# Four 32-row column tiles per expert, 32 token slots, and weight rows in 8 KB runs, in a two-block transformer kernel with 32 routed experts

## The chip, the cores and the metric

The kernel runs on one core of one Trainium2 chip. The metric is device time in microseconds (us) of one execution. TensorE does the matrix products (PE in the profile, PEld for its weight loads), VectorE is DVE, ScalarE is ACT, GpSimd is POOL, and SyncE (SP) issues nearly all transfers from HBM to the on-chip memory, the SBUF. Matrix products accumulate in PSUM.

## The reference

A first transformer block (two layers of three attention kinds) is followed by a second one with modulation vectors, banded attention, and a mixture of experts. All arithmetic is float32; 256 tokens of width 2048. The part that the change touches:

```
def hier_moe(h, w_rg, b_rg, w_re, b_re, w_gate, w_up, w_down):
    t = h.reshape(-1, D_MODEL)                       # 256 x 2048
    g_logits = t @ w_rg + b_rg                       # 4 groups, the best one is taken
    e_logits = (t @ w_re + b_re).reshape(n_tok, 4, 8)
    ...                                              # the best 2 of the 8 experts in that group
    for e in range(N_EXPERTS):                       # 32
        a = jax.nn.silu(t @ w_gate[e]) * (t @ w_up[e])
        y = y + combine[:, e:e + 1] * (a @ w_down[e])
```

Each token goes to two experts, so an expert gets 16 tokens on average. `w_gate[e]` and `w_up[e]` are 2048 x 512, `w_down[e]` is 512 x 2048, 4.19 MB each: 12.58 MB an expert, 402.7 MB in all, read once.

## The kernel before

The first block, the attention of the second and its output projection run up to about 1405 us. They split every weight into two parts and multiply three times. Beside them SP also streams the modulation matrix (`ada_gen`), which DVE multiplies. Then come the experts, one after the other.

**Slots.** A router gives each token a rank within each of its experts. Every expert has `CAP` = 64 slots. `gather` (line 1292) builds a one-hot matrix from the ranks for the two experts of a pair (2 x 64 = 128 columns), and `quarter` multiplies it with the token matrix `x`, four 128-row pieces of the model width at a time, into the tile `xg`. DVE and ACT apply norm, scale and shift, and the result is `xe` (or `xet`), the transposed input of both experts. Tokens beyond `CAP` slots are left to `overflow` (line 1393), a loop over all experts behind a branch that is taken only when some expert has more than `CAP` tokens. The branch stands after the fifth pair.

**Expert products.** `expert_gu` (line 1336) runs over 16 pieces of the model width. For each it multiplies the 64 slots with the gate piece into PSUM rows 0 to 63 and with the up piece into rows 64 to 127: two column tiles of TensorE, each with its own weights streaming through. A float32 product is two instructions in the trace. ACT copies the result out, four transposes (`guT`) turn it, and ACT and DVE form silu(gate) x up (`eth`, `aT`). `down` (line 1360) multiplies that with the four 128-row pieces of `w_down`, again in two column tiles of 64 (`acc`), and DVE scales the result into `y`. After both experts of a pair `combine` (line 1370) multiplies the 128 slot rows with the routing weights `C` (tile `cb`) and DVE adds them to the tokens' sum.

**Weights.** `load_gu` (line 1133) loads 1 MB tiles of four pieces: partition p gets rows p, 128+p, 256+p and 384+p, each a 2 KB run. `load_d` loads 512 KB tiles with 4 KB runs. There are nine 1 MB places for gate and up (an expert needs eight) and eight 512 KB places for down (an expert needs eight). SP issues the loads in one fixed order and waits, before each, until the products that used the place have run. The first 5.24 MB of expert 0 are loaded during the output projection. The order on each engine is written by a scheduler that follows the program's order within limits.

**End.** The last expert's down weights come in three column strips (line 1462), so that the final norm can follow strip by strip.

## Time and profile before

| | us |
|---|---|
| median of three runs | 2483.78 (2482.15 to 2483.81) |
| the profiled execution | 2481.46 |
| its span in the trace | 2479.8 |

The profiled execution's own time is 1.7 us above its span, and the median is 2.3 us above the profiled execution. The profile page gives busy times of each engine, 40 slices of the span, the chain of work that ended last, and the costliest groups. The trace also answers for windows: for each stretch the busy time of every engine with its number of instructions, the granted clock of TensorE (1.00 is 2.4 GHz, 0.50 is 1.2 GHz), the busy share of the 16 DMA engines (overlapping packets can bring it above 1) and the GB/s they moved.

### The profile page before, as it was taken

The numbers are of one execution on the slowest core, as the hardware profiler recorded it, in microseconds if no ns is written. First come the engines' busy times: TensorE is split into PE (matmuls) and PEld (weight loads), VectorE is DVE, ScalarE is ACT, GpSimd is POOL, SyncE is SP. The second block draws the span as 40 slices with busy tenths as digits, with TensorE's granted clock in tenths as the row PEclk, the third lists the DMA queues.
The fourth block names the chain that finished last, engine by engine and source line by source line (L and its number), as shares of the span: only waits on it lengthen the run. The fifth ranks groups of instructions, "written<-read, shape, count | busy, mean of one in ns | idle before, by whom it ended". The sixth has DMA issues, their size and how long they took to land. (4 is left out here: it accounts for less than half of the span.)

```text
span 2479.8 us, 34810 instructions
## 1 busy us (share of the span) xinstructions
PE 2344.6 (95%) x13428; PEld 1603.6 (65%) x13428; DVE 1344.5 (54%) x2207; ACT 847.7 (34%) x1727; POOL 99.3 (4%) x148
## 2 busy tenths in 40 slices
PE   8999999999999999899999899999899999999997
PEld 8998986799988877887877644333333333333342
DVE  5776867877767777867777821222222222222234
ACT  5553635555435355454565211111111111111111
POOL 0000100000100000202010000000000000000000
PEclk9999999999999999999999899999999999999998
DMA  6677986777888978769758899999999999999994
GB/s 219 221 241 249 303 280 231 271 255 234 260 263 261 290 241 280 242 234 306 250 198 298 311 358 373 394 394 394 342 394 391 393 390 389 390 394 394 394 376 177
DMA packets 340019, 760.98 MB, mean 307 GB/s; under 512 B 27628, under 2 KB 48472, under 8 KB 339848
## 3 DMA queue, kind: packets, MB, share of 16 engines
q1 hardware_dynamic: 334728, 750.92, 85.3%
q0 software_dynamic: 4928, 7.70, 1.3%
q8 instruction: 107, 1.75, 0.3%
q14 instruction: 64, 0.52, 0.1%
q10 hardware_dynamic: 192, 0.08, 0.0%
HBM read 755.69 MB, written 2.97 MB: 306 GB/s over the span
## 5 line engine op out<-in xcount | busy, mean ns | idle before, releaser
L265 ACT CAST hl<-raw 128x1024 fp32r<-128x1024 f32 (+4 forms) x478 | 423.9, 897 | 518.0 <-PE acc L290 237.5
L266 DVE TENSOR_TENSOR hl<-raw,hl 128x1024 fp32r<-128x1024 f32 (+4 forms) x478 | 485.4, 1032 | 102.9 <-ACT hl L265 102.3
L290 PE MATMUL acc<-xT,hl 128*128 128x256 f32 x3744 | 473.8, 286 | 7.7 <-DVE hl L266 4.2
L290 PEld LDWEIGHTS acc<-xT,hl 128*128 128x128 f32 x3744 | 458.0, 193 | 15.6 <-ACT hl L265 6.3
L529 DVE SCALAR_TENSOR_TENSOR ada<-raw,cact,ada 128x1024 f32<-128x1024 f32 x240 | 308.2, 1290 | 156.4 <-DMA raw<-in_w_ada_dram 138.8
L1345 PE MATMUL gu<-ew,xe 128*64 128x512 f32 x1526 | 344.1, 595 | 0.0
L1363 PE MATMUL acc<-ew,aT 128*64 128x512 f32 x992 | 237.2, 624 | 20.6 <-DVE aT L1357 20.6
L1345 PEld LDWEIGHTS gu<-ew,xe 128*64 128x64 f32 x1526 | 106.0, 137 | 203.8 <-issue 184.0
L294 PE MATMUL acc<-hl,mT 128*128 128x512 f32 x768 | 187.8, 397 | 0.6 <-DVE hl L266 0.6
L1355 DVE SCALAR_TENSOR_TENSOR eth<-eth,guT 128x256 f32<-128x256 f32 x32 | 13.5, 421 | 314.3 <-ACT eth L1354 314.3
L294 PE MATMUL acc<-hl,xT 128*128 128x512 f32 (+1 forms) x768 | 161.8, 371 | 18.1 <-DVE hl L266 17.8
L1326 PEld LDWEIGHTS xg<-oh,xres 128*128 128x128 f32 x1024 | 130.8, 196 | 72.2 <-issue 64.6
L290 PE MATMUL acc<-hT,hl 128*128 128x256 f32 x1248 | 168.9, 289 | 2.1 <-DVE hl L266 2.1
L1348 ACT COPY gus<-gu 128x512 f32<-128x512 f32 x32 | 18.8, 586 | 443.9 <-PE gu L1345 438.5
L1332 ACT ACTIVATE xe<-xe,modc 128x128 f32<-128x128 f32 x192 | 64.2, 392 | 308.7 <-DVE xe L1331 308.6
L1363 PEld LDWEIGHTS acc<-ew,aT 128*64 128x64 f32 x992 | 68.9, 142 | 148.3 <-issue 109.7
L290 PEld LDWEIGHTS acc<-hT,hl 128*128 128x128 f32 x1248 | 155.8, 192 | 12.5 <-issue 9.9
L294 PEld LDWEIGHTS acc<-hl,mT 128*128 128x128 f32 x768 | 142.1, 189 | 33.7 <-issue 4.0
L294 PEld LDWEIGHTS acc<-hl,xT 128*128 128x128 f32 x768 | 133.8, 194 | 45.3 <-DVE hl L266 23.3
L1331 DVE SCALAR_TENSOR_TENSOR xe<-xg,modc,rsb 128x128 f32<-128x128 f32 x192 | 56.2, 344 | 182.8 <-PE xg L1326 182.8
L1326 PE MATMUL xg<-oh,xres 128*128 128x128 f32 x1024 | 145.6, 287 | 5.0 <-ACT rsb L1306 5.0
L1368 DVE TENSOR_TENSOR y<-acc,gt2A 64x512 f32<-64x512 f32 x93 | 63.9, 687 | 144.4 <-PE acc L1363 142.8
(333 smaller groups left out, 2283.5 us busy)
## 6 DMA issues: line engine op xcount, KB each, us to landing
ew<-in_w_up_dram SPq DMA_DIRECT2D x128, 1024.0 KB, 11.5
ew<-in_w_down_dram SPq DMA_DIRECT2D x256, 512.0 KB, 10.2
ew<-in_w_gate_dram SPq DMA_DIRECT2D x125, 1024.0 KB, 11.7
raw<-in_w_in_dram SPq DMA_DIRECT2D x248, 512.0 KB, 5.1
raw<-in_w_ada_dram SPq DMA_DIRECT2D x192, 512.0 KB, 5.1
raw<-in_w_out_dram SPq DMA_DIRECT2D x96, 512.0 KB, 5.4
raw<-in_w_ada_final_dram SPq DMA_DIRECT2D x64, 512.0 KB, 5.9
raw<-in_w_in_dram SPq DMA_DIRECT2D x32, 256.0 KB, 3.7
```

The costliest lines, as they stand in the source:

```text
L265: A.copy(dst_hi, src)
L266: V.tensor_sub(dst_lo, src, dst_hi)
L290: T.matmul(acc[:m, b, o : o + 256], w[:, u, c : c + m], xk[v], start=st, stop=last and j == 2, skip_group_check=True)
L294: T.matmul(acc[:, b, o : o + m], xk[v][:, P * tb : P * tb + P], w[:, u, c : c + m], start=st, stop=last and j == 2, skip_group_check=True)
L529: V.scalar_tensor_tensor(ah, raw, ck, ah, op0=OP.mult, op1=OP.add)
L1326: T.matmul(ps[:, m * j : m * j + m], x[:, tb, P * k : P * k + P], oh[:, tb, :], start=j + tb == 0, stop=tb == 1, skip_group_check=True)
L1331: V.scalar_tensor_tensor(dst, ps[:, m * j : m * j + m], G2[:, k : k + 1], rs, op0=OP.mult, op1=OP.mult)
L1332: A.activation(dst, dst, AF.Identity, bias=m2[:, k : k + 1])
L1345: T.matmul(ps[64 * v : 64 * v + 64, :], xe(i, k)[:, CAP * b : CAP * b + CAP], gu(v, k), start=k == 0, stop=k == KT - 1, skip_group_check=True)
L1348: A.copy(g, ps)
L1363: T.matmul(acc[64 * (s % 2) : 64 * (s % 2) + 64, s // 2, :], aT[:, f, :], wd(f, s), start=f == 0, stop=f == 3, skip_group_check=True)
L1368: V.tensor_mul(yv(i, s)[64 * b : 64 * b + 64, :], acc[h, s // 2, :], gt2(s)[h, :])
```

## The change

`CAP` becomes 32, so four experts fill 128 columns, and the pair becomes a quad. `gather` and `combine` run once for four experts, with the same shapes as before. The gather of the next quad is asked for inside the last expert of the present one. `expert_gu` uses four column tiles of 32: gate and up, each for an even and an odd piece, so that the even and the odd sums stand in different PSUM rows. A product with the constant matrix `fold` takes the place of the four transposes: it turns the tile and adds the two sums. `down` uses four column tiles, one for each 512 columns of the output.

The model width is cut differently. Piece k no longer holds rows 128k to 128k+127 but, within each group of 512 rows, every fourth one (`quads`), so that partition p needs four neighbouring rows of `w_gate` or `w_up`, one run of 8 KB. For that the transposes of `x` before the router, the gather, the router's weights and the modulation columns use the same cut; `x` is then read in steps of four elements. `overflow` stands after the third quad and would take seven rounds an expert where it took three. Expert 0's early tiles hold 4, 4, 4, 3, 3 and 2 pieces, as many in all as before.

```
-CAP = 64
+CAP = 32
+NQ = P // CAP
...
+    def quads(t, k):
+
+        return t[..., 512 * (k // 4) : 512 * (k // 4) + 512].rearrange("p (c j) -> p j c", j=4)[:, k % 4, :]
...
+    def mod_quads(v0, gname):
+
+        rows = wk.tile([12, 512], F32, tag="stage", bufs=3, name=uid("mquad"))
+        nc.gpsimd.dma_start(rows[0:8, :], modd[v0 : v0 + 2, :].rearrange("v (m c) -> (v m) c", m=4))
+        nc.gpsimd.dma_start(rows[8:12, :], a[gname][0].rearrange("(m c) -> m c", m=4))
+        ps = pt.tile([P, 512], F32, tag="tp", name=uid("mqc"))
...
-    mod_cols(3)
+    gffn = mod_quads(3, "g_ffn_2")
     m2 = modc[3]
     G2 = modc[4]
-    V.scalar_tensor_tensor(G2, G2, 1.0, cols("g_ffn_2", KT), op0=OP.add, op1=OP.mult)
-    nc.sync.dma_start(wr[:, :, 0:4], a["w_router_group_2"][0].rearrange("(k p) n -> p k n", p=P))
-    nc.sync.dma_start(wr[:, :, 4:36], a["w_router_expert_2"][0].rearrange("(k p) n -> p k n", p=P))
+    V.scalar_tensor_tensor(G2, G2, 1.0, gffn, op0=OP.add, op1=OP.mult)
+    for c0, c1, nm in ((0, 4, "w_router_group_2"), (4, 36, "w_router_expert_2")):
+        src = a[nm][0].rearrange("(m p j) n -> p m j n", p=P, j=4)
+        for m_ in range(4):
+            nc.sync.dma_start(wr[:, 4 * m_ : 4 * m_ + 4, c0:c1], src[:, m_])
...
+    def gu_rows(w, m):
+
+        return w[512 * m : 512 * m + 512, :].rearrange("(p j) n -> p j n", j=4)
...
-            src = a[("w_gate_2", "w_up_2")[v]][0, e, P * k0 : P * (k0 + nk), :].rearrange("(k p) n -> p k n", p=P)
-            if pre:
-                t = pslot([P, nk, 512], F32, uid("ewp"))
-                nc.sync.dma_start(t, src)
-            else:
-
-                t = eload(src, [P, nk, 512], "xm" if e == 1 and k0 == 0 else None)
+            w = a[("w_gate_2", "w_up_2")[v]][0, e]
+
+            t = pslot([P, nk, 512], F32, uid("ewp")) if pre else etile([P, nk, 512], "xm" if e == 1 and k0 == 0 else None)
+            k = k0
+            while k < k0 + nk:
+                n = min(4 - k % 4, k0 + nk - k)
+                nc.sync.dma_start(t[:, k - k0 : k - k0 + n, :], gu_rows(w, k // 4)[:, k % 4 : k % 4 + n, :])
+                k += n
...
-                    T.transpose(ps[:, j, P * tb : P * tb + P], x[:, tb, P * k : P * k + P], ident)
+                    T.transpose(ps[:, j, P * tb : P * tb + P], quads(x[:, tb, :], k), ident)
...
-                    T.matmul(ps[:, m * j : m * j + m], x[:, tb, P * k : P * k + P], oh[:, tb, :], start=j + tb == 0,
+                    T.matmul(ps[:, m * j : m * j + m], quads(x[:, tb, :], k), oh[:, tb, :], start=j + tb == 0,
...
-    def expert_gu(i, b, gu, quarter=None):
+    def expert_gu(i, b, gu, quarter=None, nxt=None):
+
 
         ps = pss.tile([P, 512], F32, tag="s", name=uid("gu"))
         if quarter:
             quarter(0)
-        for k in range(KT):
+        for k in range(0, KT, 2):
             if quarter and k % 4 == 0 and k < 12:
                 quarter(k // 4 + 1)
             for v in range(2):
-                T.matmul(ps[64 * v : 64 * v + 64, :], xe(i, k)[:, CAP * b : CAP * b + CAP], gu(v, k),
-                         start=k == 0, stop=k == KT - 1, skip_group_check=True)
+                for d in range(2):
+                    c = CAP * (2 * v + d)
+                    T.matmul(ps[c : c + CAP, :], xe(i, k + d)[:, CAP * b : CAP * b + CAP], gu(v, k + d),
+                             start=k == 0, stop=k == KT - 2, skip_group_check=True)
+            if nxt and k % 4 == 2:
+                nxt(k // 4)
...
-            T.transpose(ps[:, P * f : P * f + P], g[:, P * f : P * f + P], ident)
-        v4 = ps.rearrange("p (f c) -> p f c", f=4)
+            T.matmul(ps[:, 2 * CAP * f : 2 * CAP * f + 2 * CAP], g[:, P * f : P * f + P], fold, start=f == 0, stop=True,
+                     skip_group_check=True)
+        v4 = ps[:, : 8 * CAP].rearrange("p (f c) -> p f c", f=4)
...
-    def down(acc, aT, wd, i, b, fs, ss):
-        for f in fs:
-            for s in ss:
-                T.matmul(acc[64 * (s % 2) : 64 * (s % 2) + 64, s // 2, :], aT[:, f, :], wd(f, s),
-                         start=f == 0, stop=f == 3, skip_group_check=True)
-        if fs[-1] == 3:
-            for s in ss:
-                h = slice(64 * (s % 2), 64 * (s % 2) + 64)
-                V.tensor_mul(yv(i, s)[64 * b : 64 * b + 64, :], acc[h, s // 2, :], gt2(s)[h, :])
+    def down(acc, aT, wd, i, b):
+
+        for f in range(4):
+            for s in range(4):
+                T.matmul(acc[CAP * s : CAP * s + CAP, 0, :], aT[:, f, :], wd(f, s), start=f == 0, stop=f == 3,
+                         skip_group_check=True)
+        for s in range(4):
+            h = slice(CAP * s, CAP * s + CAP)
+            V.tensor_mul(yv(i, s)[CAP * b : CAP * b + CAP, :], acc[h, 0, :], gt2(s)[h, :])
...
+    fold = cp.tile([P, 2 * CAP], F32, name="fold")
+    idq = ident.rearrange("p (v d c) -> p v d c", v=2, d=2)
+    V.tensor_add(fold.rearrange("p (v c) -> p v c", v=2), idq[:, :, 0, :], idq[:, :, 1, :])
...
-    LAST = NE // 2 - 1
-    for pr in range(LAST + 1):
-        i = pr % 2
-        C, quarter = gather(slot[:, :, 2 * pr : 2 * pr + 2], comb[:, :, 2 * pr : 2 * pr + 2], i, 2)
-        aTs = []
-        for b in range(2):
-            e = 2 * pr + b
+    def quad(q):
+        return gather(slot[:, :, NQ * q : NQ * q + NQ], comb[:, :, NQ * q : NQ * q + NQ], q % 2, NQ)
+
+    LAST = NE // NQ - 1
+    C, quarter = quad(0)
+    for q in range(LAST + 1):
+        i = q % 2
+        for b in range(NQ):
+            e = NQ * q + b
             gw = gu0 if e == 0 else gu1 if e == 1 else load_gu(e, GU) if e > 2 else {**gu2, **load_gu(2, GU[2:])}
             if e == 0:
                 gu1 = load_gu(1, GU)
                 gu2 = load_gu(2, GU[:2])
-            aT = expert_gu(i, b, lambda v, k: gw[v, k], None if b else quarter)
-            aTs.append(aT)
+            nxt = None
+            if b == NQ - 1 and q < LAST:
+                C_next, nxt = quad(q + 1)
+            aT = expert_gu(i, b, lambda v, k: gw[v, k], None if e else quarter, nxt)
...
+            if e == NE - 3:
...
-        if pr == 4:
+                combine(C, i, P, s, lambda tb: y[tb], q == 0)
+            C = C_next
+        if q == 2:
...
-        m = n // 2
+        m = n // 4
...
-            for v in range(2):
-                T.matmul(ps[64 * v : 64 * v + 64, :], aTs[1][:, f, :], wd[f // nf][:, f % nf, m * v : m * v + m], start=f == 0,
+            for v in range(4):
+                T.matmul(ps[CAP * v : CAP * v + CAP, :], aT[:, f, :], wd[f // nf][:, f % nf, m * v : m * v + m], start=f == 0,
                          stop=f == 3, skip_group_check=True)
-        for v in range(2):
```

On PE, a stretch of one expert's gate and up products before, and the transposes behind them (`gu` is the PSUM tile, `ew2409` a gate tile of four pieces, `ew2410` an up tile, `xe` the gathered input; the first two rows come four times before the next tiles' turn):

```order
L1345 MATMUL gu2415_15354<-ew2409_15342,xe2191_14248 64x512
L1345 MATMUL gu2415_15354<-ew2410_15344,xe2191_14248 64x512
...
L1345 MATMUL gu2415_15354<-ew2411_15346,xe2191_14248 64x512
L1345 MATMUL gu2415_15354<-ew2412_15348,xe2191_14248 64x512
...
L1351 MATMUL guT2417_15389<-ident_80,gus2416_15387 128x128 x4
```

The same place now (`x2` stands for two matmuls in a row; the first two rows come twice):

```order
L1376 MATMUL gu2463_15552<-ew2457_15540,xe2190_14257 32x512 x2
L1376 MATMUL gu2463_15552<-ew2458_15542,xe2190_14257 32x512 x2
...
L1376 MATMUL gu2463_15552<-ew2459_15544,xe2190_14257 32x512 x2
L1376 MATMUL gu2463_15552<-ew2460_15546,xe2190_14257 32x512 x2
...
L1384 MATMUL guT2465_15587<-fold_14284,gus2464_15585 128x64 x4
```

A weight tile still takes four matmuls, each now for 32 columns of the array instead of 64; four in a row go to four different column tiles. The four products behind them stream 64 columns instead of 128.

On PE, the end of a pair before, between the down products of its second expert (`acc`) and the first products of the next pair, with the next pair's gather (`xg`) and the combining (`cb`) between them:

```order
L1363 MATMUL acc2428_15415<-ew2427_15413,aT2419_15397 64x512 x2
L1326 MATMUL xg2452_15504<-oh2437_15460,xres_78 128x128 x5
L1373 MATMUL cb2429_15436<-y2193_14251,C2379_15165 128x512
L1373 MATMUL cb2430_15439<-y2193_14251,C2379_15165 128x512
L1326 MATMUL xg2452_15504<-oh2437_15460,xres_78 128x128 x2
L1326 MATMUL xg2453_15529<-oh2437_15460,xres_78 128x128 x2
...
L1373 MATMUL cb2436_15457<-gtB_13334,C2379_15165 128x512
L1345 MATMUL gu2450_15486<-ew2442_15470,xe2190_14247 64x512
```

The gather's new place, among the down products of a quad's third expert:

```order
L1384 MATMUL guT2465_15587<-fold_14284,gus2464_15585 128x64 x4
L1331 MATMUL rs2487_15654<-oh2485_15650,rstd2189_14205 128x128 x2
L1354 MATMUL xg2491_15669<-oh2485_15650,xres_78 128x128 x2
L1398 MATMUL acc2476_15613<-ew2468_15597,aT2467_15595 32x512 x2
L1398 MATMUL acc2476_15613<-ew2469_15599,aT2467_15595 32x512 x2
L1354 MATMUL xg2491_15669<-oh2485_15650,xres_78 128x128 x2
L1398 MATMUL acc2476_15613<-ew2470_15601,aT2467_15595 32x512 x2
L1354 MATMUL xg2491_15669<-oh2485_15650,xres_78 128x128 x4
```

The next quad's gather is done one expert before it is needed, and only the combining still stands between a quad's last down products and the next quad.

On SP, one expert's loads before:

```order
L1125 DMA ew2411_15346<-in_w_gate_2_dram 128x4x512
L1125 DMA ew2412_15348<-in_w_up_2_dram 128x4x512
L1125 DMA ew2413_15350<-in_w_gate_2_dram 128x4x512
L1125 DMA ew2414_15352<-in_w_up_2_dram 128x4x512
L1125 DMA ew2420_15399<-in_w_down_2_dram 128x1024
```

and now:

```order
L1169 DMA ew2459_15544<-in_w_gate_2_dram 128x2048
L1169 DMA ew2460_15546<-in_w_up_2_dram 128x2048
L1169 DMA ew2461_15548<-in_w_gate_2_dram 128x2048
L1169 DMA ew2462_15550<-in_w_up_2_dram 128x2048
L1148 DMA ew2468_15597<-in_w_down_2_dram 128x1024
```

Their number, size and order are the same; a gate or up load is one run of 2048 elements for each partition instead of four of 512.

## Rows read from the trace of the kernel before

**Rows 1.** The page: busy time of an engine, and the span in 40 slices.

```profile
PE 2344.6 (95%) x13428; PEld 1603.6 (65%) x13428; DVE 1344.5 (54%) x2207; ACT 847.7 (34%) x1727; POOL 99.3 (4%) x148
...
DMA  6677986777888978769758899999999999999994
GB/s 219 221 241 249 303 280 231 271 255 234 260 263 261 290 241 280 242 234 306 250 198 298 311 358 373 394 394 394 342 394 391 393 390 389 390 394 394 394 376 177
```

**Rows 2.** Windows: us, busy PE, PEld, DVE, ACT, POOL (instructions), clock, DMA share, GB/s.

```profile
1550.00:1735.00 185.00, 174.15 (x826) 71.20 (x824) 49.20 (x107) 22.18 (x61) 0.00 (x0) 1.00 1.04 394
...
1751.00:2402.00 651.00, 618.31 (x2921) 261.23 (x2921) 180.68 (x414) 81.94 (x229) 0.54 (x1) 0.98 1.03 387
```

**Rows 3.** The chain that ended last: start us, us, what.

```profile
1996.38 0.94 PE xg L1326 x6
...
2010.29 1.72 PE cb L1373 x4
...
2024.70 1.79 PE xg L1326 x16
...
2033.63 0.59 ACT gus L1348
...
2036.31 8.78 PE acc L1363 x32
2045.10 13.78 PE gu L1345 x64
...
2061.05 0.94 PE xg L1326 x6
...
2165.65 7.09 PE acc L1363 x32
```

**Rows 4.** What SP's queue waited for, 1200 to 2480: us in total, times, longest.

```profile
SPq L1125 <- PE gu L1345: 266.8, 96, 11.6
SPq L1125 <- PE acc L1363: 201.4, 172, 7.9
```

**Rows 5.** Windows of 5 us in two pairs.

```profile
2011.00:2016.00 5.00, 5.00 (x15) 2.01 (x13) 3.94 (x8) 1.34 (x4) 0.00 (x0) 1.00 1.03 411
...
2031.00:2036.00 5.00, 3.16 (x16) 0.99 (x12) 0.58 (x2) 0.97 (x2) 0.00 (x0) 1.00 1.04 358
2036.00:2041.00 5.00, 4.69 (x14) 1.44 (x16) 0.26 (x1) 0.00 (x0) 0.00 (x0) 0.66 1.05 398
...
2056.00:2061.00 5.00, 3.93 (x22) 1.63 (x18) 0.29 (x1) 1.24 (x3) 0.00 (x0) 1.00 1.05 388
...
2106.00:2111.00 5.00, 5.00 (x26) 1.69 (x24) 1.17 (x2) 0.00 (x0) 0.00 (x0) 1.00 1.04 409
```

**Rows 6.** DMA issues of the page: KB each, median us to landing.

```profile
ew<-in_w_up_dram SPq DMA_DIRECT2D x128, 1024.0 KB, 11.5
ew<-in_w_down_dram SPq DMA_DIRECT2D x256, 512.0 KB, 10.2
```

**Rows 7.** SP's timeline at the start: start us, us, line, transfer.

```profile
1403.09 2.94 SPq L1125 DMA_DIRECT2D ew<-in_w_up_dram  x3
...
1454.50 5.48 SPq L1125 DMA_DIRECT2D ew<-in_w_down_dram  x7
```

**Rows 8.** A window at the start, at the branch and at the end.

```profile
1450.00:1455.00 5.00, 5.00 (x24) 1.76 (x23) 0.84 (x2) 0.97 (x2) 0.00 (x0) 1.00 0.52 192
...
1760.00:1765.00 5.00, 5.00 (x32) 2.78 (x30) 1.08 (x4) 0.71 (x4) 0.00 (x0) 1.00 0.28 96
...
2440.00:2442.50 2.50, 2.50 (x15) 0.79 (x13) 0.00 (x0) 0.00 (x0) 0.00 (x0) 1.00 0.25 88
```

**Rows 9.** Timeline at the branch and at the end: start us, us, instruction [idle before].

```profile
1750.86 0.49 DVE L1298 TENSOR_TENSOR oh<-kk 128x128 f32<-128x128 f32 x2 [5.13 <-PEq L1398]
...
2454.70 1.41 DVE L1476 TENSOR_TENSOR y<-dn,gt2A 64x512 f32<-64x512 f32 x2 [5.45 <-PE dn L1471]
```

**Rows 10.** Groups, 1560 to 1730: the gather's weight loads, shapes, busy us, mean ns.

```profile
L1326 PEld LDWEIGHTS xg<-oh,xres 128*128 128x128 f32 x152 | 19.0, 191 | 11.3 <-issue 10.2 <-ACT rsb L1306 1.1
```

More of the change, by code (lines that the diff above doesn't have):

```diff
@@ L513, in mod_cols @@
         modc[v0], modc[v0 + 1] = t[:, 0:KT], t[:, KT : 2 * KT]
+    def quads(t, k):
[5 more added lines that the diff above has]
+        ps = pt.tile([P, 512], F32, tag="tp", name=uid("mqc"))
+        for j in range(4):
+            T.transpose(ps[:, 12 * j : 12 * j + 12], quads(rows, j), ident[:12, :12])
+        t = cp.tile([P, 48], F32, name=f"modc{v0}")
+        V.tensor_copy(t.rearrange("p (v m j) -> p j v m", v=3, m=4), ps[:, :48].rearrange("p (j v m) -> p j v m", j=4, v=3))
+        modc[v0], modc[v0 + 1] = t[:, 0:KT], t[:, KT : 2 * KT]
+        return t[:, 2 * KT : 3 * KT]
     def ada_gen():
@@ L1118, in tile_kernel, with etile @@
     wn = [0]
-    def eload(src, shape, tag=None):
+    def etile(shape, tag=None):
         if tag is None:
@@ L1123, in eload @@
             wn[0] += 1
-        t = (wk if tag == "ada" else big).tile(shape, F32, tag=tag, bufs=wbufs[tag], name=uid("ew"))
+        return (wk if tag == "ada" else big).tile(shape, F32, tag=tag, bufs=wbufs[tag], name=uid("ew"))
+    def eload(src, shape, tag=None):
+        t = etile(shape, tag)
         nc.sync.dma_start(t, src)
@@ L1306, in gather @@
         A.copy(rs, ps[:, :m])
-        C = wk.tile([m, S], F32, tag="t", bufs=3, name=uid("C"))
+        C = wk.tile([m, S], F32, tag="t" if n > 1 else "pT", bufs=3 if n > 1 else 2, name=uid("C"))
         def weights_T():
@@ L1421, in wd @@
                         return t
-                    down(accum(), aT, wd, 0, 0, range(4), range(4))
+                    down(accum(), aT, wd, 0, 0)
                     for s in range(4):
                         combine(C, 0, CAP, s, lambda tb: y[tb])
-    LAST = NE // 2 - 1
-    for pr in range(LAST + 1):
-        i = pr % 2
-        C, quarter = gather(slot[:, :, 2 * pr : 2 * pr + 2], comb[:, :, 2 * pr : 2 * pr + 2], i, 2)
-        aTs = []
-        for b in range(2):
-            e = 2 * pr + b
+    def quad(q):
[6 more added lines that the diff above has]
+            e = NQ * q + b
             gw = gu0 if e == 0 else gu1 if e == 1 else load_gu(e, GU) if e > 2 else {**gu2, **load_gu(2, GU[2:])}
@@ L1451, in tile_kernel @@
                 wd = load_d(e) if e else d0
-                down(accum(), aT, lambda f, s: wd[f, s], i, b, range(4), range(4))
-        if pr == 0:
+                down(accum(), aT, lambda f, s: wd[f, s], i, b)
+        if q == 0:
             y = [big.tile([P, D], F32, tag="xm", bufs=7, name=f"y{tb}") for tb in range(2)]
-        if pr < LAST:
+        if q < LAST:
             for s in range(4):
-                combine(C, i, P, s, lambda tb: y[tb], pr == 0)
-        if pr == 4:
+                combine(C, i, P, s, lambda tb: y[tb], q == 0)
+            C = C_next
+        if q == 2:
             overflow(y)
@@ L1469, in tile_kernel @@
         for f in range(4):
-            for v in range(2):
-                T.matmul(ps[64 * v : 64 * v + 64, :], aTs[1][:, f, :], wd[f // nf][:, f % nf, m * v : m * v + m], start=f == 0,
+            for v in range(4):
+                T.matmul(ps[CAP * v : CAP * v + CAP, :], aT[:, f, :], wd[f // nf][:, f % nf, m * v : m * v + m], start=f == 0,
                          stop=f == 3, skip_group_check=True)
-        for v in range(2):
+        for v in range(4):
             s, o = (c0 + m * v) // 512, (c0 + m * v) % 512
-            h = slice(64 * v, 64 * v + 64)
-            V.tensor_mul(yv(i, s)[64:128, o : o + m], ps[h, :], gt2(s)[h, o : o + m])
+            h = slice(CAP * v, CAP * v + CAP)
+            V.tensor_mul(yv(i, s)[P - CAP : P, o : o + m], ps[h, :], gt2(s)[h, o : o + m])
         for s in range(c0 // 512, (c0 + n) // 512):
```

10 lines of the change are left out of this document (5 added, 5 removed).

## The prediction

> **What bounds the kernel now.** I read the 40 slices first. From slice 26 on the GB/s row stands at 389 to 394 (342 once, 376 and 177 at the end), where the first 23 slices have 198 to 311 [rows 1]: the last 1050 us or so are the experts, and the change touches little else. The windows say the same without the slices' edges: from 1550 to 1735 the 16 DMA engines are never without work (share 1.04) at 394 GB/s, and from 1751 to 2402 at 387, but PE is busy 94 and 95% of these stretches too [rows 2]. Two resources are close to their limit, so I asked which of them waits for the other. The chain of waits runs through PE alone: a pair starts at 1996.38 and the next at 2061.05, 64.67 us, and every piece between is PE's or the short ACT and DVE stage between two products; no transfer is in it [rows 3]. SP waits for products to give places back, 266.8 us for `gu` and 201.4 us for `acc` [rows 4]. So PE sets the pace, and transfers follow closely: a pair is 25.17 MB, which in 64.67 us is 389 GB/s. Where PE gives places back late, the rate sinks to 358; where places are free it is 388 while gate and up tiles move (2 KB runs) and 409 to 411 while down tiles move (4 KB runs) [rows 5].
>
> So making PE faster can win only what lies between this pace and the transfers' own, plus what the longer runs add to the latter.
>
> **PE's part.** A quad of four experts is 2 x 64.67 = 129.3 us now. Its 64 gate and up matmuls an expert take 13.78 us, the 32 down matmuls 7.09, and a column tile runs beside its neighbour: 0.215 us a matmul, where a full-width one of the same 512 columns (`cb`) takes 1.72/4 = 0.43 [rows 3]. The change keeps the number of matmuls and puts four tiles side by side: I take half, 6.9 and 3.5 us. Per quad: 4 x (6.9 + 3.5) = 41.7; one gather of 64 matmuls at 1.79/16 = 0.112, 7.2; 16 combining matmuls at 1.72/4 = 0.43, 6.9; the stage from `gus` to the first `acc` (2033.63 to 2036.31) four times 2.7, 10.7; the one-hot products 1. Together 67 us, against 121 for the transfers (next part). PE comes off the path by a wide margin, so its terms weigh nothing in the sum. What they need is a cover of some 54 us per quad, and the transfers give it. If the four tiles ran only two at a time, the 41.7 would be 83 and PE would still be inside.
>
> **The transfers' part.** An expert is eight 1 MB and eight 0.5 MB loads [rows 6], 12.58 MB; 20 of expert 0's pieces (5.24 MB) are in before, so 397.4 MB are left when SP issues the rest at 1403.09 [rows 7]. The nine modulation loads queued ahead of them drain first, so I let the stream start at 1407. It ended at 2440.6, a quarter of the way into a window of 2.5 us [rows 8]: 1034 us, 384 GB/s.
>
> What do 8 KB runs give? The trace has no run of that length. One packet is one run. On one of 16 engines a 2 KB packet at 388 GB/s costs 2048 x 16 / 388 = 84.5 ns, a 4 KB one at 409 costs 160.2 ns. So each further 2 KB costs 75.8 ns and the packet itself 8.7, and an 8 KB packet would cost 311.8 ns: 420 GB/s. The bounds: nothing gained, 388; no packet cost at all, 2048 x 16 / 75.8 = 432; below, the 358 of a starved window as the worst rate of these tiles. I take 420, as the line through two measured lengths. The left 263.2 MB of gate and up need 627 us, the 134.2 MB of down at 409 need 328: 955 us, 416 GB/s on average and 121 us per quad.
>
> The page *DMA: Bandwidth & Descriptors* of the Trainium skill speaks against any of it: its Bandwidth section says that the HBM side binds transfers to SBUF at about 358 GB/s for a core, while its table of measured loads ends at 425 with 16 MB. The rows of this case pass 358 for 650 us on end [rows 2], so the measurement decides against the first figure. By the second, gate and up would need 619 us and the sum would be 8 us lower.
>
> Does the stream ever stop? Before, it did after the start, when expert 0's products came late (192 GB/s at 1450, SP's next down load at 1454.50 [rows 7, 8]), and behind the branch, where PE stood and then gathered first (96 GB/s at 1760 [rows 8]). Now expert 0's products take 6.9 us less, and the quad behind the branch has been gathered already. With PE 54 us per quad ahead, nine places for gate and up and eight for down hold 13.6 MB, over 30 us of stream; combining holds PE 7 us, and the engines stood at the branch for 5 [rows 9]. I count no stop.
>
> **Small terms.** The transposes before the router and the gather read `x` in steps of four elements. The trace has no such read; the contiguous weight load is 191 ns in the rows, overlapped to 112 per matmul [rows 3, 10]. If a step doubled that, 32 transposes and the first gather come some 12 us later, and the stream, which can run until about 1452 on the places it has, would lose up to 6 us; in later quads 7 us vanish in PE's 54. From below, nothing. I take 2 us for this and for the longer chain of the modulation columns.
>
> A rule of the Trainium skill bears on it: *SBUF — State Buffer*, section Door 1, says that each access which crosses to a new 16-byte line pays a penalty, as each of these reads does. No run here shows its size. By it the term lies toward 6, by the contiguous rows at 0.
>
> The eight router loads move the bytes of the former two beside 30 MB of other weights, and the `fold` product is no longer than the transposes; both at nothing, bounds 1 us either way.
>
> **The end.** Before, the stream ended 39 us ahead of the span's end, since PE ran an expert behind. Now PE waits for the strips. When the last expert's gate and up are in, 4.19 MB of strips (10.3 us) are still to come. PE needs about 2 us for the last piece and 2.7 for the stage, so the first strip's products start 5 us before the stream ends and take 3. From the first scaling of a strip (2454.70) to the end of the span were 25.1 us [rows 9], mostly DVE, ACT and the output's transfers; that stays, with 0.6 more for twelve scalings instead of six. So the end lies 24 us behind the stream's.
>
> **Sum.** 1407 + 2 + 955 + 24 = 2388 of span. The profiled execution was 1.7 us above its span: 2390. (The median of the runs was 2.3 above the profiled one, which is inside every bound here.)
>
> **Rivals.**
>
> *A, the runs give nothing.* Packets at 2 and 4 KB differ by 5% in rate, but down tiles differ from the others in more than run length, and places were freer when they moved. Then gate and up stay at 388: 678 + 328 = 1006, 51 us more, 2442.
>
> *B, TensorE falls to half its clock.* Behind the 5 us window with PE idle a third of the time, the granted clock was 0.66 and the down products took 8.78 instead of 7.09 us [rows 3, 5]. Now PE idles half of every quad. Were it at 1.2 GHz throughout, 83 + 14.3 + 13.8 + 10.7 + 2 = 124 us per quad, 3 more than the transfers: 8 x 3 = 24, so 2414. Against it: while PE is busy without gaps the rows show 1.00, and at 124 of 121 it would have no gaps.
>
> *C, the long runs are slower.* The span breaks even when the stream takes 2480 - 1407 - 2 - 24 = 1047, that is 719 for gate and up, 366 GB/s. From there down the change loses; at 350 it is 2390 + 752 - 627 = 2515. For it: four times fewer packets in flight, and short supply did cost rate in the 358 window. Against: from 2 to 4 KB the rate rose.
>
> *D, column tiles take turns.* If the array streamed one tile of 32 at a time, a quad would be 165 + 26 = 191 us and the kernel about 2390 + 8 x 70 = 2950; the change loses from 129 us per quad on. Two tiles of 64 run fully beside each other, so I give it little.
>
> *E, the overflow runs.* Counting the experts' tokens in the reference for its default draw gives 26 at most, six under the new 32. Were one above, 32 x 7 x 12.58 MB at 394 GB/s are 7 ms more.
>
> **How the numbers follow.** Forecast 62%, its own range 2376 to 2405 (425 with no loss, or 412 and the 6 us). A 15%, B 10%, still better than the forecast 3%, no change 2%, C 5%, D 2%, E 1%. About 0.2% is what a measurement of this kernel can tell from no change, 5 us. Faster 0.90, same 0.02, slower 0.08. The range goes from 2376 to 2445: it takes in A and B and leaves out the better case and C to E.
>
> **What would show it.** Right: the expert stage has share above 1 throughout and about 415 GB/s; windows with gate and up tiles alone show about 420, those with down 409; packets of 8 KB appear; PE is busy about half of the stage and its waits name DMA; SP waits for landings, not for products; the stream ends near 2364 and the span 24 us later. `gu` takes about 108 ns per matmul. The granted clock swings between the levels. Wrong: a rate at 394 is A; PE back on the chain at 0.50 is B; a rate under 388 in gate and up windows is C.

## The result and the profile after

The changed kernel takes 2394.18 us (median of four runs, 2391.18 to 2397.79) where the kernel before, run beside it, took 2482.97: ratio 0.9652, 95% interval 0.9624 to 0.968. Its profiled execution, the fastest of the four, took 2391.18 us with a span of 2389.5. The forecast was 2390 us with a range of 2376 to 2445.

The page of the changed kernel, with the lines that answer to [rows 1]: PE's busy time, the slices, and the packets.

```profile
PE 2117.2 (89%) x12919; PEld 1483.5 (62%) x12919; DVE 1253.8 (52%) x1990; ACT 794.8 (33%) x1583; POOL 100.0 (4%) x149
...
GB/s 227 221 227 252 306 296 246 235 255 266 221 267 270 303 300 220 223 332 202 297 222 244 304 345 369 417 417 416 417 416 417 417 417 417 417 417 417 416 417 255
DMA packets 242079, 760.90 MB, mean 318 GB/s; under 512 B 27760, under 2 KB 48572, under 8 KB 209400
```

From slice 26 on the GB/s row is flat until the last slice. The last count is of packets under 8 KB, so 32,679 packets have 8 KB or more. Each gate or up run is such a packet now, but for those of expert 0's cut tiles.

Windows in the expert stage, columns as in [rows 2]:

```profile
1550.00:1735.00 185.00, 142.28 (x732) 52.66 (x731) 29.52 (x65) 12.45 (x35) 0.00 (x0) 0.93 1.02 417
1751.00:2350.00 599.00, 466.03 (x2461) 167.83 (x2455) 125.03 (x252) 44.88 (x120) 0.54 (x1) 0.92 1.02 417
```

The stream runs at 417 GB/s on both sides of the branch, where before it had 394 and 387 with PE 94 to 95% busy. PE is busy 77 and 78% of these stretches.

What SP's queue waited for from 1460 to 2365 (columns as in [rows 4]):

```profile
SPq L1148 <- DMA ew<-in_w_up_dram: 251.2, 119, 2.8
SPq L1148 <- DMA ew<-in_w_gate_dram: 249.7, 119, 2.8
SPq L1169 <- DMA ew<-in_w_down_dram: 204.0, 230, 1.2
SPq L1169 <- PE acc L1398: 6.9, 22, 0.4
SPq L1169 <- PE gu L1376: 3.7, 8, 1.4
```

This is the change in one view. SP waited 468 us for products before [rows 4], 442 of them from 1460 to 2440; now its waits name the landing of earlier transfers, in pieces of 1 to 3 us, and products add up to less than 20. Places are free in time, and the DMA engines are what is waited for.

The chain that ended last, in the stage, answering to [rows 3]:

```profile
1839.46 10.12 DMA ew<-in_w_down_dram
...
1849.65 20.53 DMA ew<-in_w_up_dram
...
1870.24 10.17 DMA ew<-in_w_down_dram
...
1941.01 19.81 DMA ew<-in_w_up_dram
...
1983.93 0.98 PE acc L1398 x4
...
1986.87 3.46 PE xg L1354 x14
1990.33 7.07 PE gu L1376 x64
```

An expert is 8.39 MB of gate and up in about 20 us and 4.19 MB of down in about 10.15. PE still enters the chain at a quad's end (1961 to 2002), and two things can be read there. The 64 `gu` matmuls take 7.07 us, 110 ns each, where [rows 3] have 13.78: four column tiles run fully beside each other. And 14 gather matmuls take 3.46 us, 0.247 each, where [rows 3] have 0.112: reading `x` at a step of 16 bytes more than doubled them.

The one place where the stream stops is the first quad, as in [rows 8]:

```profile
1425.00:1430.00 5.00, 5.00 (x30) 3.44 (x30) 1.13 (x4) 1.28 (x4) 0.00 (x0) 1.00 0.90 346
...
1440.00:1445.00 5.00, 5.00 (x46) 1.98 (x42) 0.57 (x2) 0.86 (x2) 0.00 (x0) 1.00 0.65 224
1445.00:1450.00 5.00, 5.00 (x52) 1.52 (x48) 1.71 (x3) 0.00 (x0) 0.00 (x0) 1.00 0.65 201
1450.00:1455.00 5.00, 4.25 (x38) 1.73 (x30) 1.03 (x2) 0.58 (x1) 0.00 (x0) 1.00 1.00 318
```

Added up over the six windows from 1425 to 1455 (346, 372, 388, 224, 201, 318 against 417), 3.3 MB are missing, 7.8 us of stream. The window at 1760 (96 GB/s in [rows 8]) has no counterpart.

### The profile page after: what moved, and what is told of

Its sections match the earlier page's. It is cut to its first block, busy times and chain, and to the rows that moved or that the text cites. A ratio compares the mean times of both kernels' runs of the same rounds, so it can differ in the third digit from the quotient of the medians.

```text
span 2389.5 us, 33378 instructions
## 1 busy us (share of the span) xinstructions
PE 2117.2 (89%) x12919; PEld 1483.5 (62%) x12919; DVE 1253.8 (52%) x1990; ACT 794.8 (33%) x1583; POOL 100.0 (4%) x149
## 5 line engine op out<-in xcount | busy, mean ns | idle before, releaser
L1376 PE MATMUL gu<-ew,xe 128*32 128x512 f32 x1528 | 249.1, 657 | 100.5 <-DMA ew<-in_w_up_dram 62.2
L1389 DVE SCALAR_TENSOR_TENSOR eth<-eth,guT 128x128 f32<-128x128 f32 x32 | 9.2, 288 | 437.2 <-ACT eth L1388 437.2
L1376 PEld LDWEIGHTS gu<-ew,xe 128*32 128x32 f32 x1528 | 52.6, 114 | 281.1 <-DMA ew<-in_w_up_dram 110.0
L1398 PE MATMUL acc<-ew,aT 128*32 128x512 f32 x992 | 180.1, 693 | 25.9 <-DVE aT L1391 22.2
L1354 PEld LDWEIGHTS xg<-oh,xres 128*128 128x128 f32 x512 | 123.9, 327 | 40.7 <-issue 30.2
L1402 DVE TENSOR_TENSOR y<-acc,gt2A 32x512 f32<-32x512 f32 x93 | 63.6, 684 | 147.9 <-PE acc L1398 146.9
L1354 PE MATMUL xg<-oh,xres 128*128 128x128 f32 x512 | 134.8, 409 | 2.6 <-ACT rsb L1334 2.1
L1376 PE MATMUL gu<-ew,xet 128*32 128x512 f32 x504 | 93.6, 651 | 33.3 <-DMA ew<-in_w_up_dram 26.8
L1398 PEld LDWEIGHTS acc<-ew,aT 128*32 128x32 f32 x992 | 35.3, 121 | 112.9 <-issue 48.2
L295 PE MATMUL acc<-hl,oT 128*128 128x512 f32 x384 | 97.7, 401 | 0.0
```

What stands on the lines that cost most here:

```text
L295: T.matmul(acc[:, b, o : o + m], xk[v][:, P * tb : P * tb + P], w[:, u, c : c + m], start=st, stop=last and j == 2, skip_group_check=True)
L1354: T.matmul(ps[:, m * j : m * j + m], quads(x[:, tb, :], k), oh[:, tb, :], start=j + tb == 0, stop=tb == 1, skip_group_check=True)
L1376: T.matmul(ps[c : c + CAP, :], xe(i, k + d)[:, CAP * b : CAP * b + CAP], gu(v, k + d), start=k == 0, stop=k == KT - 2, skip_group_check=True)
L1389: V.scalar_tensor_tensor(th, th, 1.0, v4[:, :, 0:CAP], op0=OP.add, op1=OP.mult)
L1398: T.matmul(acc[CAP * s : CAP * s + CAP, 0, :], aT[:, f, :], wd(f, s), start=f == 0, stop=f == 3, skip_group_check=True)
L1402: V.tensor_mul(yv(i, s)[CAP * b : CAP * b + CAP, :], acc[h, 0, :], gt2(s)[h, :])
```

## The experiments

**A yardstick first.** Profiled executions reach the first product behind the router (`rank`) at different times, from 1413 to 1425 us. Six of the kernels below have the same program up to there (the changed one, its repetition, e3, e4, e7 and e8), and they lie up to 5.3 us apart. Two executions of the very same code, the changed kernel and its repetition, differ by 3.5 us, and SP's first expert load differs with them:

```profile
1394.48 1.38 SPq L1169 DMA_DIRECT2D ew<-in_w_up_dram  x3
...
1415.74 0.24 PE L1266 MATMUL rank<-rscr,kk 128*128 128x64 bf16 x1 [3.20 <-DVE rscr L1264]
```

```profile
1397.83 1.42 SPq L1169 DMA_DIRECT2D ew<-in_w_up_dram  x3
...
1419.20 0.24 PE L1266 MATMUL rank<-rscr,kk 128*128 128x64 bf16 x1 [3.20 <-DVE rscr L1264]
```

In every kernel of the table that load comes 21.3 to 21.8 us ahead of `rank`, so `rank` marks the start of the stream as well. Beside the timed ratio I therefore give the length from this product to the end of the span, called the stage.

| kernel | median us | ratio to before (95%) | stage us |
|---|---|---|---|
| before | 2482.97 | | 1055.0 |
| changed | 2394.18 | 0.9652 (0.9624 to 0.968) | 973.8 |
| changed, again | 2394.06 | 0.9657 (0.9633 to 0.9681) | 971.6 |
| e1 tiles and quads, old row order | 2442.2 | 0.9856 (0.9834 to 0.9878) | 1022.6 |
| e2 new row order alone | 2599.81 | 1.0472 (1.0453 to 1.049) | 1177.5 |
| e3 two column tiles for gate and up | 2405.11 | 0.9703 (0.9681 to 0.9724) | 983.5 |
| e4 gather of whole blocks | 2391.96 | 0.9642 (0.9619 to 0.9664) | 969.7 |
| e5 4 KB runs | 2405.07 | 0.9696 (0.9666 to 0.9725) | 981.7 |
| e6 x reordered | 2393.18 | 0.9651 (0.9618 to 0.9683) | 969.3 |
| e7 down in 8 KB too | 2386.91 | 0.9626 (0.9591 to 0.9661) | 964.5 |
| e8 one expert's down for all | 2196.54 | 0.8862 (0.8829 to 0.8896) | 768.6 |
| e9 x reordered, places kept | 2392.22 | 0.9634 (0.9615 to 0.9652) | 968.1 |
| e10 e9 and e7 together | 2384.27 | 0.9615 (0.9592 to 0.9639) | 961.0 |
| e11 e8 with reordered x | 2132.3 | 0.8601 (0.8582 to 0.862) | 710.7 |

**e1, all of the change but the row order.** The 32 slots, the quads, the earlier gather and the column tiles stay; the long runs go.

```diff
-        return w[512 * m : 512 * m + 512, :].rearrange("(p j) n -> p j n", j=4)
+        return w[512 * m : 512 * m + 512, :].rearrange("(j p) n -> p j n", j=4)
```

(`quads` and the router's loads likewise.)

> The changed kernel with the rows in the old order: gate and up in runs of 2 KB, x read in whole blocks; the 32 slots, four column tiles and quads stay. Theory (PE off the path and run length each give a part): the stream runs without stops from about 1407 at the rates of the kernel before where it did not wait, 388 GB/s for gate and up and 411 for down: 264.9 MB / 0.388 + 132.5 MB / 0.411 = 1005 us, plus 24 us of tail, 2436 span, about 2438 us. The gather's weight loads fall back from 327 to about 190 ns and its matmuls to about 0.11 us. Rival 'it is all PE, the runs give nothing': 2388 to 2394. Rival 'it is all the runs': about 2483.

2442.2 us, 4 us above the expected sum for both parts. It is also the case that rival A of the prediction prices, gate and up at the rate of 2 KB runs. The stream runs without the first quad's stop (387 to 408 GB/s in every window from 1425 to 1455), but at the old rate:

```profile
1751.00:2350.00 599.00, 435.02 (x2337) 133.23 (x2333) 120.62 (x247) 45.24 (x122) 0.54 (x1) 0.92 1.04 394
```

**e2, the row order alone.** Its edits are made in the kernel before, with pairs, 64 slots and two column tiles: 8 KB runs, and `x` read at a step of 16 bytes.

> The kernel before with the rows in the new order alone: 64 slots, pairs, two column tiles at a time, but gate and up in runs of 8 KB and x read at a step of 16 bytes. Theory: PE sets the pace of a pair (64.7 us against 60.3 for its 25.2 MB at 417 GB/s), so the longer runs can give nothing, and the strided gather adds 64 x (0.247 - 0.112) = 8.6 us to each pair's PE chain: 16 x 8.6 = 138 us, 2580 to 2620 us, slower than before; PE busy nearly all of the stage, SP waiting for products. Rival 'the runs alone give the gain': about 2394. Rival 'the strided reads are hidden beside other PE work': 2470 to 2485.

2599.81 us, 4.7% slower. PE sets the pace (busy 94% of the window, and SP waits 763 us for products), the stream falls to 348, and the gather, which here runs once in every pair, has weight loads of 326 ns in place of 191 [rows 10]:

```profile
1751.00:2350.00 599.00, 562.90 (x2362) 271.20 (x2360) 147.32 (x333) 64.30 (x179) 0.54 (x1) 0.98 0.89 348
```

```profile
L1353 PEld LDWEIGHTS xg<-oh,xres 128*128 128x128 f32 x1024 | 251.6, 326 | 67.5 <-issue 55.0
```

SP's waits from 1460 to 2560:

```profile
SPq L1168 <- PE gu L1372: 543.0, 121, 20.1
SPq L1147 <- PE acc L1390: 220.1, 194, 9.8
```

The stage is 122 us longer than before, 138 were expected from the gather alone. So the two halves of the change don't add up: everything but the row order is worth 32 us of stage, the row order alone costs 122, both together gain 81. The row order is worth 49 us once PE is off the path. No run has the long runs on the old schedule with whole-block reads; that the slow gather makes up the loss is read from its own times.

Nor does a run tell the tiles from the quads. An estimate from the rows: the tiles take 4 x (13.78 - 7.07) + 4 x (7.09 - 3.5) = 41 us of PE out of a quad, and one gather and one combining in place of two take out 14, of which the step gives 8 back.

**e3, two column tiles in place of four.**

```diff
-            for v in range(2):
-                for d in range(2):
-                    c = CAP * (2 * v + d)
+            for d in range(2):
+                for v in range(2):
+                    c = CAP * v
...
```

(The down products keep their four tiles.)

> The changed kernel with gate and up accumulated in two column tiles in place of four (one for gate, one for up, each over all 16 feature blocks; the fold becomes a plain transpose). Theory: the 64 matmuls of an expert take 13.8 us in place of 7.1, PE per quad about 77 + 27 = 104 us against 121 of transfers: the time stays within 10 us of the changed kernel's 2394 (the first quad, which PE sets, starts about 10 us later), the stream still at 415 or more in the middle. Rival 'PE is near the bound, at its lowered clock above all': over 2440, the stream below 400 GB/s. Rival 'four tiles do not run beside each other any better than two': the 64 matmuls take 7 us here too.

2405.11 us, 11 us more than the changed kernel. In the middle of the stage the stream has 415 all the same. The windows from 1430 to 1460 (218, 387, 216, 233, 188, 113) miss 13.8 us of stream, 6 more than in the changed kernel: at the first quad PE sets the pace.

```profile
1450.00:1455.00 5.00, 5.00 (x28) 1.93 (x26) 0.57 (x2) 0.85 (x2) 0.00 (x0) 1.00 0.46 188
1455.00:1460.00 5.00, 5.00 (x42) 1.91 (x40) 0.70 (x2) 0.00 (x0) 0.00 (x0) 1.00 0.44 113
...
1751.00:2350.00 599.00, 526.42 (x2477) 203.43 (x2481) 127.40 (x260) 48.02 (x130) 0.54 (x1) 0.98 1.02 415
```

So doubling the time of gate and up on PE costs little, 10 to 12 us of stage, and by the windows about half of that at the start.

**e4, the gather reads whole blocks.**

```diff
-                    T.matmul(ps[:, m * j : m * j + m], quads(x[:, tb, :], k), oh[:, tb, :], ...
+                    T.matmul(ps[:, m * j : m * j + m], x[:, tb, P * k : P * k + P], oh[:, tb, :], ...
```

> The changed kernel with the gather reading whole blocks of 128 columns of x instead of every fourth column; the experts then get the wrong features, so the output is not the reference's, but every instruction and byte stays. Theory: the reads at a step of 16 bytes are what makes the gather's matmuls 0.247 us instead of 0.112; the first quad's gather takes 7.2 us in place of 15.6, the stop of the stream between 1428 and 1450 shrinks by about 6 to 8 us and the end comes 5 to 8 us earlier: 2386 to 2389. The later quads change nothing, they are hidden. Rival 'the stop at the start comes from the router's work, not the gather': 2394, unchanged. Rival 'the slow gather costs at every quad change': 7 x 8.6 = 60 us less, 2334.

By the median 2 us less, not 5 to 8, and the intervals overlap: the time shows no difference. The mechanism is there, its size is off. The gather's matmuls from PE's timeline, first the changed kernel, then e4:

```profile
1418.13 7.55 PE L1354 MATMUL xg<-oh,xres 128*128 128x128 f32 x32
...
1427.47 4.00 PE L1354 MATMUL xg<-oh,xres 128*128 128x128 f32 x16
...
1433.53 3.89 PE L1354 MATMUL xg<-oh,xres 128*128 128x128 f32 x16
```

```profile
1423.03 6.06 PE L1354 MATMUL xg<-oh,xres 128*128 128x128 f32 x32
...
1430.88 2.05 PE L1354 MATMUL xg<-oh,xres 128*128 128x128 f32 x16
...
1434.99 1.95 PE L1354 MATMUL xg<-oh,xres 128*128 128x128 f32 x16
```

With whole blocks the gather is 10.1 us in place of 15.4, but not 7.2: its first 32 products took 6.06, and the granted clock was 0.50 from 1420 to 1425 and 0.71 in the next 5 us. The stop shrinks to 2.7 us (247 and 360 GB/s in the windows from 1445). The profiled execution came to the stage 4.9 us later than the changed kernel's, which weighs against it in the time; the stage is 2 to 4 us shorter, hardly more than the two profiles of the changed kernel differ. Nothing changed at later quads (417 as before): that rival is out.

**e5, runs of 4 KB.** Two neighbouring rows per partition: `rearrange("(h p j) n -> p h (j n)", p=P, j=2)`.

> The changed kernel with two neighbouring rows in each partition in place of four: gate and up in runs of 4 KB, x read at every second column (a step of 8 bytes). Theory (the run's length sets the rate of gate and up): between the 394 GB/s overall of 2 KB and the 417 of 8 KB, at the rate that down has with its 4 KB runs, 409 to 413 GB/s for all: 397.4 MB / 0.411 = 967 us, +1407 + 24 + a stop of 0 to 8 us, 2400 to 2406 us. Rival 'it is the place of the rows and not the run': 2394 or 2442. For the gather: if the price of its weight loads goes with the step, something between 190 and 327 ns; if it is one fixed price for any step, 327 ns again.

2405.07 us, as expected. With e1 and e7 this gives the rate against the run. The DMA view of 1600 to 1700 in e1, e5, the changed kernel and e7:

```profile
DMA packets 16590, 39.47 MB, mean 395 GB/s; under 512 B 821, under 2 KB 821, under 8 KB 16586
```

```profile
DMA packets 10805, 40.91 MB, mean 409 GB/s; under 512 B 829, under 2 KB 829, under 8 KB 10801
```

```profile
DMA packets 7739, 41.72 MB, mean 417 GB/s; under 512 B 861, under 2 KB 861, under 8 KB 4439
```

```profile
DMA packets 5777, 42.09 MB, mean 421 GB/s; under 512 B 642, under 2 KB 642, under 8 KB 642
```

The bytes come in fewer packets and faster; between the first three only the order of the rows differs, and with it the step at which `x` is read. The gather at a step of 8 bytes has weight loads of 197 ns (median), beside 192 for whole blocks and 329 for 16 bytes: the price comes with the last step, not evenly.

**e6, x reordered once.** The projection's first half writes `x` in the order of the weights' rows by a copy on ScalarE; transposes and gather read whole blocks; the end adds `x` into `y`.

```diff
+                V.tensor_add(u, xs, u)
+                A.copy(plain(xs)[:, 0], rowsj(u)[:, 0])
...
```

> The changed kernel, same output, with x put in the order of the weights' rows once: the first half of the output projection's sum writes x in the new order by an extra copy on ScalarE, eight in all, the second half adds at a step, and the router's transposes and the gather read whole blocks; the end adds x into y. Theory: as with plain blocks in the gather, the first quad's gather falls from 15.4 us to 7 to 10 and the stop of the stream after 1425 from 7.8 us (worked out from its windows) to about 3; the transposes' weight loads gain too; the copies lie beside TensorE's work: 4 to 6 us less than the changed kernel, 2387 to 2390. Rival 'the additions at a step and the copies delay the last strip and the router by as much': 2394 or more.

2393.18 us, nearer the rival's 2394 than the theory's 2387 to 2390. The first stop shrank to 2.4 us, but a new one stands near the end, which e4 doesn't have:

```profile
2335.00:2340.00 5.00, 2.74 (x12) 0.53 (x14) 2.24 (x4) 0.00 (x0) 0.00 (x0) 0.80 0.60 252
2340.00:2345.00 5.00, 2.12 (x12) 0.37 (x6) 0.00 (x0) 0.00 (x0) 0.00 (x0) 0.84 0.75 259
```

Two rows of the final norm are allocated there. They used to get the two 8 KB places of `y`, which is alive to the end now, so they took two of the five that rotate, and the last expert's gate load waited.

**e7, the down weights in whole rows.**

```diff
+        for f in range(4 if 0 < e < NE - 1 else 0):
+            t = eload(a["w_down_2"][0, e, P * f : P * f + P, :], [P, D])
...
```

> The changed kernel with the down weights of experts 1 to 30 in whole rows too (runs of 8 KB, 1 MB tiles), which fit only in the nine 8 KB places of gate and up; the eight 4 KB places stand empty, so about 9.4 MB are loaded ahead in place of 13.6. Theory 'the rate goes with the run': down from about 413 to 421 GB/s, 125.8 MB in 299 us in place of 305, 6 us less, 2388. Rival 'the places ahead matter more': 22 us of load ahead against some 23 us that gather and combine put into the expert before a quad's end; the stream stops at each of the seven changes for up to 10 us, 2400 to 2460. I hold the second a little likelier.

2386.91 us, with an interval that overlaps that of the changed kernel, and a stage 7 to 9 us shorter. That is the first theory, though I had held the second likelier; the second's 2400 to 2460 is out. Places do run out, as SP's waits from 1460 to 2365 show, but the transfers already queued nearly bridge it, at 418 GB/s in place of 421:

```profile
SPq L1169 <- PE acc L1402: 154.6, 63, 7.9
SPq L1148 <- PE gu L1380: 148.4, 66, 15.9
SPq L1169 <- DMA ew<-in_w_down_dram: 110.7, 81, 2.8
```

```profile
1751.00:2350.00 599.00, 450.74 (x2469) 162.64 (x2461) 124.98 (x252) 44.51 (x120) 0.54 (x1) 0.92 1.01 418
```

**e8, no down loads for experts 1 to 30.**

```diff
-                wd = load_d(e) if e else d0
+                wd = d0
```

> The changed kernel with the down weights of experts 1 to 30 not loaded: all of them use expert 0's, so the output is not the reference's, and 125.8 MB of 397 are left out, with every product kept. Theory (the transfers set the pace, PE has some 40 us per quad to spare): the time falls by nearly what the bytes took, 125.8 MB / 0.413 = 305 us, to about 2090, unless PE's own work, 8 quads of about 77 us and some 20 of dependences, is reached first: 2090 to 2130. Rival 'PE or the waits between engines set the pace': a fall of less than 200 us, over 2190.

2196.54 us: a fall of 198, so my number is refuted and the rival's (less than 200) is met. A third of the bytes gone gives two thirds of their time. The end of the fourth quad shows where the rest went:

```profile
1780.00:1790.00 10.00, 9.18 (x55) 5.82 (x53) 1.99 (x8) 3.27 (x11) 0.00 (x0) 1.00 0.85 335
1790.00:1800.00 10.00, 7.40 (x37) 2.02 (x37) 4.15 (x8) 0.24 (x1) 0.00 (x0) 0.83 0.71 301
1800.00:1810.00 10.00, 10.00 (x56) 3.15 (x60) 4.60 (x7) 0.00 (x0) 0.00 (x0) 1.00 0.14 29
```

While the next gather runs beside the last expert's products, and then through the down products and the combining, PE gives places back slowly: SP can issue eight loads, 8.4 MB, between 1757.07 and 1807.60, and none between 1788.12 and 1807.60. Together with nine full gate and up places that is 17.8 MB, where the stream at 417 GB/s would move 21. (At the third quad's end the branch adds to it, with 5 GB/s from 1700 to 1710.) Between the quads' ends PE isn't the bound; from 1430 to 2150 it waits for landings:

```profile
PE gu L1376 <- DMA ew<-in_w_up_dram: 29.1, 23, 1.4
PE gu L1376 <- DMA ew<-in_w_gate_dram: 11.9, 18, 1.8
```

**e9 and e11, the reordered x with the places kept; e10, with the down rows as well.** The norm's two rows now lie in the old place of `x`:

```diff
-                gf, hf = [big.tile([P, D], F32, tag="xm", bufs=7, name=n) for n in ("gf", "hf")]
+                gf, hf = x[:, 0, :], x[:, 1, :]
```

> The reordered x once more (same output as the reference), with one thing set right: there the two rows of the final norm took two of the five rotating 8 KB places that y had given back before, and the stream stopped at 2335 to 2345 (252 and 259 GB/s). Now they lie in the old place of x, which is free by then, and the result leaves from y. Theory: the stop near the end goes (3.8 us), the shorter stop at the first quad stays (2.4 us in place of 7.8), 2387 to 2390 where the changed kernel has 2394. Rival 'the start of the stage moves by as much from run to run, or the additions at a step delay the router': 2392 to 2396, not to be told from the changed kernel.

> The kernel that uses expert 0's down weights for all (126 MB left out, output not the reference's), with the reordered x, so that each quad's gather is short. There the time fell by 198 us and not by 305, and the trace showed the stream at 5 to 30 GB/s for some 10 us at each quad's end. Theory: what stops it there is PE, which with gather, combine and the quad's last expert is some 15 us behind, longer than the nine places cover; each quad's gather takes about 8 us less now, so 7 to 8 times up to 8 us go: 2196 to about 2135 to 2145. Rival 'the bound there is the transfers' own rate or the length of PE's work over a whole quad with its waits': less than 25 us of gain.

> The same with the down weights in whole rows of 8 KB as well. Theory: the two gains add up, since one is at the start and the other in the rate (422 in place of 417 GB/s), and the shorter gather leaves the nine places more time at the quads' ends, where 418 was reached in place of 421: 2376 to 2383, the fastest so far. Rival 'the stream's end is set by the nine places once down is in them': 2386, as with the down rows alone.

e11 fits this reading of e8: 2132.3 us, 64 less, with a gather that is some 8 us shorter in each of eight quads. It lies slightly below the expected 2135 to 2145; a stop at the quads' ends remains, 85 GB/s from 1850 to 1860. A kernel that PE bounds all the time would have gained as much, so against that stand e8's waits for landings and not this number. e9 has 2392.22 us, the rival's number, which can't be told from the changed kernel by time; its stage is 3.5 to 5.7 us shorter, and the late stop is gone (417 from 1751 to 2350). e10 has 2384.27 us, above the expected 2376 to 2383 but the lowest of all with the full output, and a stage 11 to 13 us shorter than the changed kernel's. Its runs spread from 2375.68 to 2395.58 and its interval just overlaps that of the changed kernel, so the gain in time is likely and not shown; the shorter stage rests on one profile each.

**e12, the changed kernel again.**

> The changed kernel itself once more, since the profiled executions reach the router's rank product at 1413 to 1425 us, with nothing altered before it. From that product to the end the first profile took 973.8 us; plain gather 969.7, reordered x 968.1, down in 8 KB 964.5, both 961.0. Theory 'the stretch before the stage moves from execution to execution, the stage itself does not': 972 to 976 from the rank product to the end again, wherever that product falls, and a median of 2391 to 2397. Rival 'the stage varies as well, and differences of 4 to 13 us between these kernels are chance': a stretch that is off by 4 us or more.

971.6 us of stage, 0.4 below the expected span of values, with `rank` 3.5 us later than in the first profile. Its stop at the first quad is 7.5 us (344, 364, 328, 164, 322, 355 in the windows from 1430 to 1460). So the stage repeats within some 2 us in these two profiles, and e4's 969.7 alone is not far enough from that to count.

## Why the prediction came out right

**The bound.** Right. SP's waits turned from products to landings, and where PE is covered the time follows the rate of the stream (e1, e5, the changed kernel).

**PE's part.** Right in its conclusion, low in its sum. The matmuls took 110 ns against the 108 predicted, but the gather took 15.4 us per quad in place of 7.2, so a quad is about 77 us of PE, not 67. PE busy was 77%, not about half; 77 of 121 us would be 64%, and the granted clock of 0.92 accounts for a part of the rest only, the remainder stays open. The average of 54 us of cover was also the wrong yardstick. What e8 shows to count is the stretch in which few places are given back against what the places hold: 13.6 MB were enough for it, e8's nine places were not.

**The transfers' part.** Right. The line through the 2 and 4 KB packets gave 311.8 ns for 8 KB; e7's 421 GB/s, with all tiles in such runs, are 311 ns. The whole stream ran at 417 where 416 was predicted. As to the two figures of the Trainium skill (*DMA: Bandwidth & Descriptors*, section Bandwidth), 417 GB/s over the two stretches of 784 us together passes the 358 once more, and the 425 at which its table ends was not reached. The same section gives its measured loads as those of one core with the pair's other core idle, and the 358 as each core's part with both streaming; this kernel runs on one core.

**The small terms.** The step that failed is "I count no stop" together with the 2 us for the strided reads: there were 7.8 us, above the upper bound of 6. The bound supposed that a step at most doubles the 0.112 us of a gather matmul; 0.247 were measured. The stop has a second part that no bound covered: whole blocks (e4, e6) still leave 2.4 to 2.7 us. The transposes, which the term counted too, have weight loads of 209 ns in place of 141, and no delay shows for it: from the first load to `rank` it is 21.3 us in the changed kernel and 21.7 before. The rule on 16-byte lines (*SBUF — State Buffer*, section Door 1, of the Trainium skill) agrees with the gather's 329 ns at a step of 16 bytes. It asks for at least two hits per line, which a step of 8 bytes gives, and the 197 ns there agree as well; a size it doesn't state.

**The end.** Predicted 24 us behind the stream's end, measured 27.6: the stream ended near 2361.9 (158 of 421 GB/s in the window from 2360). The first strip's 32 products started at 2359.10, only 3 us ahead of that, and took 3.51 us at the lower clock in place of 3:

```profile
2359.10 3.51 PE L1515 MATMUL dn<-ew,aT 128*32 128x256 f32 x32 [1.01 <-DVE aT L1391]
...
2362.69 1.75 DVE L1520 TENSOR_TENSOR y<-dn,gt2A 32x256 f32<-32x256 f32 x4 [3.65 <-PE dn L1515]
```

**The sum.** Measured: 397.4 MB at 417 are 953 us (955 predicted), 7.8 of stop (2) and 27.6 of end (24); what is left of 2389.5 is a start at 1401 (1407). Six us of error in the small terms and 3.6 at the end were made good by the earlier start, so that the total is better than its parts is luck. Of the start, 3.4 us is the spread between two executions of the same kernel (1394.48 and 1397.83 for the first load); before, that load stood at 1403.09 [rows 7], and whether the change moved it the runs don't show. The lower end of the forecast's own range, 2376, does not follow from what it names: 425 for gate and up and no loss give 2380.

**The rivals.** A is out by 417 GB/s; e1, at 2442.2, shows that its price of 2442 was right. B did not come: the granted clock was 0.92 to 0.93 over the two stretches of the stage, near the upper level. C, D and E are out by 417 GB/s, by 110 ns and by the time itself. What none of them said is e2: the same row order on the old PE schedule costs 118 us.

## What to carry to other kernels

Where two resources are near their limits, the halves of a change can be worth more together than their sum, and one half alone less than nothing: build each alone before you credit it. Compare the longest stretch in which a consumer gives few buffers back with what the buffers hold, not averages per period. A layout that lengthens the transfers' runs is read by somebody at a step: price that read too, above all where the consumer is not yet hidden.

## What the runs showed of the hardware that I had not expected

- The gather's weight loads of 128x128 fp32 take 192 ns from whole blocks (e4), 197 at a step of 8 bytes (e5) and 329 at 16, by the median. Those of the transposes before the router rise less at 16 bytes, from 141 to 209.
- In e6 a DVE addition of 128x512 fp32 that reads and writes `x` at a step of 512 bytes took 1074 ns in place of 684, and an ACT copy of that size that writes so 1133, where contiguous squares of it take 630 on ACT.
- The rate of a stream that never waits is 388 GB/s at 2 KB runs (e1, 1425 to 1435), 409 at 4 KB (e5) and 421 at 8 KB (e7, 1600 to 1700).
- The same instructions before the stage ended up to 5.3 us apart among the profiled executions of six kernels; the runs don't show why.
